# The openings and closings of two feed-forward blocks put into one written order

## The chip, the cores and the metric

One core of a Trainium2 chip. The metric is device time in microseconds (us) of one execution, the median of several runs. The core has TensorE (PE, the matmuls; PEld is its loading of weights), VectorE (DVE), ScalarE (ACT), GpSimd (POOL), and SyncE (SP), which here issues most DMAs. Each engine works through its own queue in order; semaphores hold an instruction until what it reads is there and what it overwrites has been read.

## The reference

One layer of an encoder over 768 tokens (a prompt of 512 and a sample of 256), model width 1024:

```python
def encoder_layer(x, ...):
    x = layer_norm(ALPHA * x + 0.5 * swiglu(x, ffn1_up, ffn1_down), ln1_g, ln1_b)
    u = x @ w_in
    ...                       # RWKV-7 branch h_a, retention branch h_b, gates
    x = layer_norm(ALPHA * x + mix, ln2_g, ln2_b)
    x = layer_norm(ALPHA * x + 0.5 * swiglu(x, ffn2_up, ffn2_down), ln3_g, ln3_b)
    return x

def swiglu(x, w_up, w_down):
    gate, up = jnp.split(x @ w_up, 2, axis=-1)
    return (jax.nn.silu(gate) * up) @ w_down
```

`w_up` is 1024 x 5632, `w_down` 2816 x 1024, `w_in` 1024 wide on its input side, all in float32.

## The kernel before

**Tiles.** Activations lie transposed: 128 features on the partitions, tokens along the free axis. `z[0..7]` are the eight tiles of x, 128 x 768. A float32 product is made of three matmuls on pieces: a high part (a CAST on ScalarE: xh, ph, wh, hh) and the low rest (a subtraction on VectorE: xl, pl, wl, hl), high x high, high x low and low x high. `split` makes both parts; `mmt` (L208) issues the matmuls.

**The up products.** The 2816 hidden features are 22 blocks, numbered j. A block needs a gate and an up column of weights, each in two halves of 512 inputs, against x in two halves of inputs and two halves of 384 tokens. Instead of eight half products the kernel makes seven (Strassen's way): products 1 and 2 take the gate weights as loaded and x as it is ("11", "21"); products 5, 7, 6, 3 take sums of weights (`combine`, tile sa, L359), and products 4 to 7 differences of x, the forms "T1" to "T4" (tiles f, L293, then split into xh, xl, eh, el); product 3 takes "22". Each product is 12 matmuls of 128 x 384 into a PSUM bank (tile pc). ScalarE copies or applies silu (u, L367, L374, L415, L421), VectorE adds products up (L410), multiplies gate by up (L427), and the result is split into hh (L432) and hl (L436).

**The down products.** The blocks are grouped in `CHUNKS` of 6, 6, 5 and 5. The down products of the first three groups are mixed into the up products of the next; those of the last group (`last_down`, L567 adds them to z) come at the end, first for the 512 prompt tokens ("segment 0"), then for the 256 of the sample ("segment 1"), for the eight output tiles n. The group's weights (tiles w) are loaded and split for segment 0; what still has a place is kept for segment 1, and five of the eight are loaded and split again. The first two outputs are begun before the last block's hh is there.

**The order.** `ffn` builds a list of items, one for each product. Inside `manual_schedule` the three compute engines keep the order in which `body` writes the instructions: at step t the additions of item t-1, loads for up to `AHEAD` = 9 items ahead, weight sums, then `prep(t + 2)`, which casts and subtracts the weights of item t+2, then the matmuls of item t. What stands outside, the opening and the closing, is put in order by the scheduler's own estimates of time. The opening: `first` loads x and makes the forms; `head` and `second` make products 1 and 2 of the first `LEAD` = 4 blocks, so that their matmuls run while the forms are made; the other five products of these blocks are items. The closing: `last_down`, then `layer_norm` for each segment: a sum over features by a matmul with ones (L253, L262), centring (L273), squares (L275), their sum, the root (`rsqrt`, table load L234, then L240 to L244), scaling (L281), an affine on ScalarE (L282) and, after the first block, the split into xh and xl for the next stage.

**What follows the first block.** Two products of x with `w_in` columns 12 and 13, the "lead" tiles, are begun in the closing (`project`). The next stage takes their PSUM tiles over: L703 to L707 read them into t and r, and the projections of that stage use a ring of three PSUM tiles (mm), the two lead tiles and one of their own. `mmps` counts through this ring with `self.turn`, which starts at -1, so that the first tile given out is the first lead's.

Of the kernel before, what the change touches and what calls it, by code (L numbers as in the profile page):

```python
# [18 lines left out]
P = 128  # L19
# [36 lines left out]
LEAD = 4  # L56
RAWS = 10
AHEAD = 9
# [11 lines left out]
class Builder:  # L70
# [165 lines left out]
    def rsqrt(self, p, eps, o, t, last):  # L236
        nc = self.nc
        last = self.lntable(last)
        with self.tc.issue_after(last):
            nc.scalar.activation(o, p, AF.Ln, bias=eps)  # L240
# [49 lines left out]
    def forms(self, z, xs, ext, tmp):  # L290
        nc = self.nc
        m = KT // 2
        sub = lambda o, a, b: nc.vector.tensor_tensor(out=o, in0=a, in1=b, op=ALU.subtract)  # L293
        B = [[t[:, c:c + TH] for t in (z[k], z[k + m]) for c in (0, TH)] for k in range(m)]
        ta = [tmp.tile([P, T], F32, tag="hh", name=self.nm("f")) for k in range(m)]
        for k, (b11, b12, b21, b22) in enumerate(B):
            sub(ta[k][:, :TH], b12, b11)
            self.split(ta[k][:, :TH], *(t[:, TH:] for t in xs[k]))
        tb = [tmp.tile([P, T], F32, tag="hl", name=self.nm("f")) for k in range(m)]
        for k, (b11, b12, b21, b22) in enumerate(B):  # L300
            sub(tb[k][:, :TH], b22, b12)
            self.split(tb[k][:, :TH], *(t[:, :TH] for t in ext[k]))
        for k, (b11, b12, b21, b22) in enumerate(B):
            sub(ta[k][:, TH:], b22, ta[k][:, :TH])
            self.split(ta[k][:, TH:], *(t[:, 2 * TH:] for t in ext[k]))
        for k, (b11, b12, b21, b22) in enumerate(B):
            sub(tb[k][:, TH:], b21, ta[k][:, TH:])
            self.split(tb[k][:, TH:], *(t[:, TH:2 * TH] for t in ext[k]))

    def ffn(self, ctx, z, xs, idx, up, down, after, lead, first, then=None):  # L310
# [6 lines left out]
        hs, raws, open_ = {}, {}, {}  # L317
# [25 lines left out]
        def load(j, part):  # L343
            if (j, part) not in raws:
                raws[j, part] = raw(up[j, :, part])
            return raws[j, part]

        def pieces(src):
            n = src.shape[-1]
            h, l = (fw.tile([P, m * P], F32R, tag=t, name=self.nm(t), bufs=4)[:, :n] for t in ("ph", "pl"))  # L350
            self.split(src, h, l)
            return tuple(t.rearrange("p (a b) -> p a b", b=P) for t in (h, l))

        def product(ps, w, x, start):
            self.mmt(ps, self.terms(pieces(w), X[x]), ((0, TH),), start, True, not start)

        def combine(a, b, op):
            t = fw.tile([P, m * P], F32, tag="sa", name=self.nm("sa"), bufs=4)
            nc.vector.tensor_tensor(out=t, in0=a, in1=b, op=op)  # L359
            return t  # L360

        def head(j):
            g = load(j, 0)
            s, uu = (hp.tile([P, T], F32, tag=t, name=self.nm("u")) for t in ("hh", "hl"))
            ps = self.bank()[:, :TH]
            product(ps, g[0], "11", True)
            nc.scalar.copy(uu[:, :TH], ps)  # L367
            open_[j] = s, uu, ps
            return g

        def second(j, g):
            s, uu, ps = open_[j]
            product(ps, g[1], "21", False)
            nc.scalar.activation(s[:, :TH], ps, AF.Silu)  # L374

        def pair_items(j):
            early = j in open_
            st = {}

            def sums(names):  # L380
                def run():
                    (g0, g1), (u0, u1) = load(j, 0), load(j, 1)
                    for n in names:
                        if n == 1:
                            st[1] = combine(u0, u1, ALU.add)
                        elif n == 3:
                            st[3] = combine(g0, u0, ALU.subtract)
                        elif n == 2:
                            st[2] = combine(st[1], g0, ALU.subtract)
                        else:  # L390
                            st[4] = combine(g1, st[2], ALU.subtract)
                return run

            if early:
                st["s"], st["u"] = open_[j][:2]
# [5 lines left out]
            def bank_of(n):  # L401
                key = {1: "A", 2: "A", 5: "C", 3: "C", 7: "D", 4: "D", 6: "B"}[n]
                if key not in st:
                    st[key] = self.bank()[:, :TH]
                return st[key]

            src = {1: lambda: load(j, 0)[0], 2: lambda: load(j, 0)[1], 4: lambda: load(j, 1)[1],
# [26 lines left out]
            def after_late(n):  # L434
                if n == 4:
                    nc.vector.tensor_tensor(out=hs[j][1], in0=st["s"], in1=hs[j][0].bitcast(F32), op=ALU.subtract)  # L436
                    for k in ((j, 0), (j, 1)):
                        raws.pop(k)

            items = []  # L440
            of = {5: 1, 7: 3, 6: 2, 3: 4}
            for n in (5, 7, 6, 3, 4) if early else (1, 5, 7, 6, 2, 3, 4):
# [4 lines left out]
                need = (sums((of[n],)), 3 if early else 6 + (n in (6, 3))) if n in of else None  # L447
                items.append((src[n], mm, *(lambda n=n, f=f: f(n) for f in (post, late, after_late)), need))
# [908 lines left out]
```

## Time and profile before

| what | us |
|---|---|
| median of 3 runs | 1986.06 (1985.82 to 1988.34) |
| the profiled execution | 1982.73 |
| its span | 1981.0 |
| PE busy in the span | 1886.8 |
| DVE busy | 1259.4 |
| ACT busy | 807.0 |

The profile is one execution; its span runs from the first to the last instruction, and 1.73 us lie around it. A line number names a line of the kernel, often that of a helper, so the tile beside it says what the work is. "PE pc L208 <- ACT u L367" in the table of waits means that matmuls into pc waited for ScalarE's copy of u. A number in brackets after x counts instructions. The granted clock is TensorE's, 1.00 at full speed. Times of stages: the first block runs from 0 to about 582 with its closing from about 488, the second from about 1430 to the end with its closing from about 1908.

### The profile page before, as it was taken

What the parts mean: (1) busy time and instruction counts of PE and PEld (TensorE: products, weight loads), DVE (VectorE), ACT (ScalarE), POOL (GpSimd) and SP (SyncE); (2) the same over time, 40 slices, a digit from 0 to 9 for tenths busy, and PEclk for the clock granted to TensorE, in tenths of its full rate; (3) what the DMA queues carried; (4) which work ended last, traced back from release to release, by engine and by line L of the source; (5) the groups of instructions that cost most, each with busy time, mean ns of one, the idle gap of its engine ahead of it and who ended that gap; (6) DMA issues with size and microseconds to landing.
All of it is one profiled execution on the core that took longest, in us unless ns stands there. A gap on an engine that the chain in (4) does not pass through costs nothing.

```text
span 1981.0 us, 33145 instructions
## 1 busy us (share of the span) xinstructions
PE 1886.8 (95%) x13098; PEld 1685.0 (85%) x13098; DVE 1259.4 (64%) x2208; ACT 807.0 (41%) x1521; POOL 190.3 (10%) x290
## 2 busy tenths in 40 slices
PE   7999999999989999999899989999899999999997
PEld 7999999998778778887688867789789899899985
DVE  8855746656745686768445555386797477375655
ACT  6422423323454353545255555332554234132325
POOL 0000000000000365345610000000000000000000
PEclk9999999999989999999999989999999999999998
DMA  5222222121332433333555442654222221222221
GB/s 197 81 69 75 64 75 71 49 85 45 123 103 69 156 115 127 116 128 121 155 164 139 123 121 74 210 163 138 80 77 73 81 69 56 79 63 69 67 70 66
DMA packets 140444, 198.40 MB, mean 100 GB/s; under 512 B 55552, under 2 KB 73600, under 8 KB 140288
## 3 DMA queue, kind: packets, MB, share of 16 engines
q1 hardware_dynamic: 122752, 174.25, 27.8%
q0 software_dynamic: 3424, 14.94, 2.2%
q10 hardware_dynamic: 14112, 7.08, 1.3%
q8 instruction: 104, 1.70, 0.4%
q14 instruction: 52, 0.43, 0.1%
HBM read 154.54 MB, written 41.68 MB: 99 GB/s over the span
## 4 chain that ended last, share of the span: by engine, by line
PE 82%; DVE 9%; ACT 4%; DMA 3%; issue 2%; SPq 0%; ACTq 0%; POOL 0%; DVEq 0%; POOLq 0%
PE mm L208 39%; PE pc L208 30%; PE pc L253 2%; PE mm L630 2%; PE pc L107 2%; PE pc L1046 1%; DMA t<-gd 1%; PE w L982 1%; PE pc L1094 1%; PE pc L687 1%; DVE z L281 1%; PE w L993 1%; DVE u L410 1%; PE w L987 1%; PE pc L1055 1%
## 5 line engine op out<-in xcount | busy, mean ns | idle before, releaser
L208 PE MATMUL pc<-xh,ph 128*128 128x384 f32 x704 | 241.9, 344 | 20.8 <-ACT u L367 6.7
L208 PE MATMUL pc<-xl,ph 128*128 128x384 f32 x704 | 237.8, 338 | 0.1
L197 ACT CAST ph<-wr 128x512 fp32r<-128x512 f32 (+1 forms) x232 | 131.1, 568 | 220.2 <-PE mm L208 140.3
L208 PE MATMUL mm<-xh,wh 128*128 128x512 f32 (+1 forms) x640 | 177.2, 356 | 15.0 <-DVE t L707 5.1
L410 DVE TENSOR_TENSOR u<-u,pc 128x384 f32<-128x384 f32 x220 | 121.6, 553 | 89.1 <-PE pc L208 85.4
L208 PE MATMUL pc<-el,ph 128*128 128x384 f32 x528 | 176.4, 334 | 0.0
L208 PE MATMUL pc<-eh,ph 128*128 128x384 f32 x528 | 176.4, 334 | 0.0
L208 PE MATMUL mm<-xl,wh 128*128 128x512 f32 (+1 forms) x640 | 169.9, 346 | 0.0
L208 PEld LDWEIGHTS pc<-xh,ph 128*128 128x128 f32 x704 | 133.7, 190 | 30.4 <-ACT u L367 8.0
L198 DVE TENSOR_TENSOR pl<-wr,ph 128x512 fp32r<-128x512 f32 (+1 forms) x232 | 141.6, 623 | 20.6 <-ACT ph L197 20.6
L208 PE MATMUL pc<-xh,pl 128*128 128x384 f32 x704 | 151.0, 336 | 0.0
L198 DVE TENSOR_TENSOR pl<-sa,ph 128x512 fp32r<-128x512 f32 x176 | 121.2, 689 | 45.6 <-ACT ph L197 45.4
L208 PE MATMUL mm<-hl,ph 128*128 128x512 f32 (+1 forms) x544 | 138.9, 336 | 0.0
L208 PE MATMUL mm<-hh,ph 128*128 128x512 f32 (+1 forms) x544 | 138.8, 336 | 0.0
L208 PEld LDWEIGHTS pc<-xl,ph 128*128 128x128 f32 x704 | 133.8, 190 | 0.8 <-DVE xl L198 0.7
L169 DVE TENSOR_TENSOR wl<-wr,wh 128x1024 fp32r<-128x1024 f32 (+1 forms) x68 | 74.8, 1100 | 92.7 <-PE mm L208 47.2
L208 PEld LDWEIGHTS mm<-xh,wh 128*128 128x128 f32 x640 | 101.7, 192 | 36.9 <-issue 14.9
L197 ACT CAST ph<-sa 128x512 fp32r<-128x512 f32 x176 | 105.4, 617 | 52.9 <-DVE sa L359 24.9
L208 PEld LDWEIGHTS pc<-xh,pl 128*128 128x128 f32 x704 | 125.7, 189 | 0.0
L208 PE MATMUL mm<-xh,wl 128*128 128x512 f32 (+1 forms) x640 | 124.2, 343 | 0.0
L168 ACT CAST wh<-wr 128x1024 fp32r<-128x1024 f32 (+1 forms) x68 | 62.7, 922 | 139.0 <-PE mm L208 112.7
L208 PEld LDWEIGHTS mm<-xl,wh 128*128 128x128 f32 x640 | 100.6, 192 | 16.8 <-issue 2.5
(311 smaller groups left out, 3926.3 us busy)
## 6 DMA issues: line engine op xcount, KB each, us to landing
wr<-in_f1u SPq DMA_DIRECT2D x96, 256.0 KB, 3.1
wr<-in_f2u SPq DMA_DIRECT2D x96, 256.0 KB, 3.0
wr<-in_w_in SPq DMA_DIRECT2D x30, 512.0 KB, 3.5
wr<-in_f1d SPq DMA_DIRECT2D x37, 256.0 KB, 2.7
wr<-in_f2d SPq DMA_DIRECT2D x37, 256.0 KB, 2.7
wr<-in_w_in SPq DMA_DIRECT2D x32, 256.0 KB, 3.4
dd<-ar SPq DMA_DIRECT2D x8, 768.0 KB, 3.3
dd<-kb SPq DMA_DIRECT2D x8, 768.0 KB, 4.4
```

The lines of the kernel that those rows point to most:

```text
L107: self.nc.tensor.matmul(ps, w, x[:, a:b], start=True, stop=True)
L168: nc.scalar.copy(hi, raw)
L169: nc.vector.tensor_tensor(out=lo, in0=raw, in1=hi.bitcast(F32), op=ALU.subtract)
L197: self.nc.scalar.copy(hi, src)
L198: self.nc.vector.tensor_tensor(out=lo, in0=src, in1=hi.bitcast(F32), op=ALU.subtract)
L208: self.latest = self.nc.tensor.matmul(o, w, x[:, a:b], start=start and i == 0, stop=stop and i == len(terms) - 1, skip_group_check=more).ins
L253: self.summed = nc.tensor.matmul(st["ps"], self.ones, src, start=k == 0, stop=k == KT - 1).ins
L281: nc.vector.scalar_tensor_tensor(out=zk, in0=zk, scalar=-0.5, in1=rs, op0=ALU.mult, op1=ALU.mult)
L410: add = lambda o, a, b: nc.vector.tensor_tensor(out=o, in0=a, in1=b, op=ALU.add)
L630: nc.tensor.matmul(dst, x[:, ts], w[:, :, k % 4], start=(k == 0 and q == 0), stop=(k == KT - 1 and q == 2))
L687: nc.tensor.matmul(op, v[:, a // P + j], x[:, j, :n], start=(j == 0 and q == 0), stop=(j == nj - 1 and q == 2))
L982: nc.tensor.matmul(pb[64 * h:64 * h + 64, C * j:C * j + C], sc[:, c % 4, h, 1], vu[:, c % 4, h], start=True, stop=True)
```

## The change

1. The opening of both blocks goes into the item list. `LEAD` is 6: the twelve products 1 and 2 of six blocks come first in the order `OPEN`; then the blocks go in pairs, with products 5, 7, 6 of both alternating, and then 3 and 4 of each. Product 6 of these six blocks uses an mm tile of PSUM instead of a pc bank. The gate weights are loaded half by half, in the first block mixed with quarters of x (`inputs`).
2. `forms` no longer runs at once: it returns a list of steps, and `advance(t)` writes a few of them behind each item's weights, up to three VectorE operations at a time, or more where item t needs them.
3. `prep` is split: ScalarE casts the weights of item t+3 (`high`) when VectorE makes the low part of item t+2. `AHEAD` is 10.
4. `closing` takes the place of `last_down`, `layer_norm` and the code of `project` in `first`, and is written inside `manual_schedule`. The 24 matmuls of outputs 0 and 1 that don't need the last block stand behind the last up product. The last group's weights are split once: for three outputs into hp tiles, for four into the tiles of the forms (xe, free by then), and the eighth into what is left of those. Sums, centring, squares, root, scaling and `project` are written between the products of segment 1.
5. The constants for the next stage are loaded at item 100 (`then`) instead of behind the last item. The affines of outputs 3 and 6 of segment 1 in the second block are on VectorE. `psum` starts `turn` at `len(pre) - 1`, so that the first tile given out is the pool's own, not the first lead's.

The number and the shapes of the matmuls are the same; VectorE has 17 operations fewer, ScalarE 24, SP 20 loads fewer in the first block's up weights, and 8 more in the second's.

```diff
-LEAD = 4
+LEAD = 6
+OPEN = [(1, 0), (1, 1), (1, 2), (1, 3), (2, 0), (2, 1), (1, 4), (1, 5), (2, 2), (2, 3), (2, 4), (2, 5)]
+FORMS = {True: 5, False: 6}
-AHEAD = 9
+AHEAD = 10
...
-        self.pre, self.turn = pre, -1
+        self.pre, self.turn = pre, len(pre) - 1
...
+            early = [pair_items(j) for j in range(LEAD)]
+            items += [early[j][0][n] for n, j in OPEN]
+            for j in range(0, LEAD, 2):
+                pair = early[j:j + 2]
+                fetch.setdefault(len(items), []).extend(p[1] for p in pair)
+                items += [p[0][n] for n in (5, 7, 6) for p in pair] + [p[0][n] for p in pair for n in (3, 4)]
...
+            def advance(t):
+                x = items[t][7] if 0 <= t < len(items) else None
+                names = [n for n, *_ in steps]
+                must = len(names) - names[::-1].index(x) if x in names else 0
+                begin = FORMS[own]
+                n = 0
+                while steps and (must > 0 or n < (3 if t >= begin else 0) or steps[0][0] == "11"
+                                 or steps[0][0] == "21" and t >= 0 and n < 2):
...
             def prep(t):
-                if t < len(items):
-                    ready[t] = pieces(items[t][0]())
+                if t + 1 < len(items):
+                    ready[t + 1] = high(items[t + 1][0]())
+                if 0 <= t < len(items):
+                    ready[t] = pieces(*ready[t])
...
+        def closing(out, lead):
...
+            for n in range(2):
+                ps[n] = self.mmps()
+                product(SEGS[0], n, range(nk - 1), True, False)
...
+            for n in range(KT):
+                if n == 0:
+                    add(0, KT - 1)
+                ps[n] = self.mmps()
+                product(SEGS[1], n, range(nk), True, True)
+                if n == 0:
+                    total(0)
+                elif n < 5:
+                    centre(0, 2 * n - 2)
+                    centre(0, 2 * n - 1)
+                if n > 1:
+                    total(1, n - 2)
+                if 1 < n < 6:
+                    square_sum(0, 2 * n - 4)
+                    square_sum(0, 2 * n - 3)
+                if n:
+                    add(1, n - 1)
+                if n == 5:
+                    root(0)
+                if n > 5:
+                    scale(0, 2 * n - 12)
+                    scale(0, 2 * n - 11)
+                if n == 7 and lead:
+                    low(0, 0)
+                    low(0, 1)
+            add(1, KT - 1)
+            total(1, KT - 2)
+            total(1, KT - 1)
```

VectorE at the start of the first block, before (pl: low part of a weight tile, xl: of a tile of x, f: a form):

```order
L198 TENSOR_TENSOR pl_227<-wr_119,ph_226 128x512
L198 TENSOR_TENSOR pl_244<-wr_121,ph_243 128x512
L198 TENSOR_TENSOR xl_87<-z_78,xh_86 128x384
L198 TENSOR_TENSOR xl_89<-z_79,xh_88 128x384
L198 TENSOR_TENSOR xl_91<-z_80,xh_90 128x384
L198 TENSOR_TENSOR xl_93<-z_81,xh_92 128x384
L198 TENSOR_TENSOR xl_95<-z_82,xh_94 128x384
L198 TENSOR_TENSOR xl_97<-z_83,xh_96 128x384
L198 TENSOR_TENSOR xl_99<-z_84,xh_98 128x384
L198 TENSOR_TENSOR xl_101<-z_85,xh_100 128x384
L198 TENSOR_TENSOR pl_264<-wr_147,ph_263 128x512
```

And now:

```order
L313 TENSOR_TENSOR xl_87<-z_78,xh_86 128x384
L313 TENSOR_TENSOR xl_89<-z_79,xh_88 128x384
L313 TENSOR_TENSOR xl_91<-z_80,xh_90 128x384
L313 TENSOR_TENSOR xl_93<-z_81,xh_92 128x384
L376 TENSOR_TENSOR pl_175<-wr_119,ph_163 128x512
L376 TENSOR_TENSOR pl_179<-wr_125,ph_173 128x512
L376 TENSOR_TENSOR pl_183<-wr_127,ph_177 128x512
L313 TENSOR_TENSOR xl_95<-z_82,xh_94 128x384
L313 TENSOR_TENSOR xl_97<-z_83,xh_96 128x384
L376 TENSOR_TENSOR pl_210<-wr_129,ph_181 128x512
L313 TENSOR_TENSOR xl_99<-z_84,xh_98 128x384
L376 TENSOR_TENSOR pl_244<-wr_135,ph_208 128x512
```

The low parts of the first weights now stand between the pieces of x: three gate products that need only the lower half of x come ahead of the pieces of the upper half.

VectorE at the root of segment 0 in the closing of the second block, before (z<-z,mm: a product added to z; sa: the root; z<-z,sa: scaling; z<-z,pc: centring):

```order
L242 TENSOR_TENSOR sa_19134<-sa_19133 128x512
L567 TENSOR_TENSOR z_13012<-z_13012,mm_19286 128x256
L243 SCALAR_TENSOR_TENSOR sa_19134<-pc_19100,eps,sa_19134 128x512
L244 SCALAR_TENSOR_TENSOR sa_19133<-sa_19134,sa_19133 128x512
L281 SCALAR_TENSOR_TENSOR z_13010<-z_13010,sa_19133 128x512
L281 SCALAR_TENSOR_TENSOR z_13011<-z_13011,sa_19133 128x512
L281 SCALAR_TENSOR_TENSOR z_13012<-z_13012,sa_19133 128x512
L281 SCALAR_TENSOR_TENSOR z_13013<-z_13013,sa_19133 128x512
L281 SCALAR_TENSOR_TENSOR z_13014<-z_13014,sa_19133 128x512
L281 SCALAR_TENSOR_TENSOR z_13015<-z_13015,sa_19133 128x512
L281 SCALAR_TENSOR_TENSOR z_13016<-z_13016,sa_19133 128x512
L281 SCALAR_TENSOR_TENSOR z_13017<-z_13017,sa_19133 128x512
```

And now:

```order
L243 TENSOR_TENSOR sa_19169<-sa_19168 128x512
L244 SCALAR_TENSOR_TENSOR sa_19169<-pc_19026,eps,sa_19169 128x512
L245 SCALAR_TENSOR_TENSOR sa_19168<-sa_19169,sa_19168 128x512
L602 TENSOR_TENSOR z_12954<-z_12954,mm_19148 128x256
L634 SCALAR_TENSOR_TENSOR z_12949<-z_12949,sa_19168 128x512
L634 SCALAR_TENSOR_TENSOR z_12950<-z_12950,sa_19168 128x512
L602 TENSOR_TENSOR z_12955<-z_12955,mm_19175 128x256
L634 SCALAR_TENSOR_TENSOR z_12951<-z_12951,sa_19168 128x512
L634 SCALAR_TENSOR_TENSOR z_12952<-z_12952,sa_19168 128x512
L602 TENSOR_TENSOR z_12956<-z_12956,mm_19199 128x256
L634 SCALAR_TENSOR_TENSOR z_12953<-z_12953,sa_19168 128x512
```

Before, all eight scalings of segment 0 came in a row, with two additions of segment 1 behind them. Now the additions of the last three outputs stand between the scalings, and five scalings come ahead of segment 1's centring; the other three stand behind it (not shown).

ScalarE in the closing of the first block, before (z<-z,vec: the affine; xh: the high part of the next stage's x; the rows begin at the root's last step):

```order
L241 ACTIVATE sa_4926<-sa_4926 128x512
L282 ACTIVATE z_78<-z_78,vec_4640 128x512
L282 ACTIVATE z_79<-z_79,vec_4640 128x512
L197 CAST xh_4877<-z_78 128x512
L282 ACTIVATE z_80<-z_80,vec_4640 128x512
L197 CAST xh_4879<-z_79 128x512
L282 ACTIVATE z_81<-z_81,vec_4640 128x512
L282 ACTIVATE z_82<-z_82,vec_4640 128x512
L197 CAST xh_4881<-z_80 128x512
```

And now:

```order
L242 ACTIVATE sa_5046<-sa_5046 128x512
L644 ACTIVATE z_78<-z_78,vec_2419 128x512
L647 CAST xh_4663<-z_78 128x512
L644 ACTIVATE z_79<-z_79,vec_2419 128x512
L647 CAST xh_4665<-z_79 128x512
L644 ACTIVATE z_80<-z_80,vec_2419 128x512
L647 CAST xh_4667<-z_80 128x512
L644 ACTIVATE z_81<-z_81,vec_2419 128x512
L170 CAST wh_5409<-wr_5408 128x1024
L647 CAST xh_4669<-z_81 128x512
L644 ACTIVATE z_82<-z_82,vec_2419 128x512
L199 CAST wh_5470<-wr_5469 128x1024
```

Each high part now follows its affine at once, and two casts of the next stage's weights (wh), which stood ahead of the root before, stand among them.

More of the change, by code (lines that the diff above doesn't have):

```diff
@@ L303, in forms @@
[L303 to L310, printed above, removed]
+        part = lambda ts, k, c: tuple(t[:, c:c + TH] for t in ts[k])
@@ new lines, in forms, with low, begin @@
+        if own:
+            rows += [("22", None, B[k][3], part(xs, k + m, TH)) for k in range(m)]
+        rows += [("T4", tt(tb[k], B[k][2], tb[k], ALU.subtract), tb[k], part(ext, k, TH)) for k in range(m)]
+        steps, late = [], None
+        def low(src, hi, lo):
+            return lambda: nc.vector.tensor_tensor(out=lo, in0=src, in1=hi.bitcast(F32), op=ALU.subtract)
+        for name, make, src, (hi, lo) in rows:
+            def begin(make=make, src=src, hi=hi):
+                if make:
+                    make()
+                nc.scalar.copy(hi, src)
+            if late and name == "21" != late[0]:
+                steps.append(late)
+                late = None
+            steps.append((name, begin, bool(make), False))
+            if late:
+                steps.append(late)
+            late = name, low(src, hi, lo), True, True
@@ L311, in ffn @@
+        return steps + [late]
+    def ffn(self, ctx, z, xs, idx, up, down, out, lead, start, own, then=None):
         nc = self.nc
@@ L354, in product @@
[L354 to L359, printed above, removed]
-            return t
[L362 to L374, printed above, removed]
+        def load(j, part, h):
+            if (j, part, h) not in raws:
+                raws[j, part, h], = raw(up[j, :, part, h * m:h * m + m])
+            return raws[j, part, h]
+        def high(src):
+            h = fw.tile([P, m * P], F32R, tag="ph", name=self.nm("ph"), bufs=4)[:, :src.shape[-1]]
+            nc.scalar.copy(h, src)
+            return src, h
@@ L497, in body @@
                     fetch.setdefault(len(items), []).append(get)
[L498 to L499 removed]
+                    items += [its[n] for n in (1, 5, 7, 6, 2, 3, 4)]
                     if q == 0 and ci:
[L501 to L504 removed]
+                        items += down_items(ci - 1)
@@ L539, in body @@
                 for f in afters:
                     f()
+                ahead(t)
+                if then and t == 100:
+                    with self.tc.issue_after(self.mark):
+                        then()
+                for f in extra.get(t, ()):
+                    f()
+                prep(t + 2)
+                advance(t)
+                if t > 0:
+                    items[t - 1][3]()
+                    afters = [items[t - 1][4]]
+                if 0 <= t < len(items):
+                    items[t][1](ready.pop(t))
@@ L548, in last_down @@
+        def closing(out, lead):
             ch = chunks[-1]
-            a, b = seg
-            mean = {"ps": self.bank()[:, :b - a]}
-            order = [n for n in held] + [n for n in range(KT) if n not in held]
-            now = dict(held)
+            nk = len(ch)
             x = [hs[j] for j in ch]
-            part = lambda ps, w, c, *ends: self.mmt(ps, self.terms([t[:, c] for t in w], x[c]), (seg,), *ends)
-            begun = {n: self.mmps() for n in order[:2]} if a == 0 else {}
-            for n, ps in begun.items():
-                part(ps, now[n], slice(0, len(ch) - 1), True, False)
@@ L569, in last_down @@
-            return mean, {n: now[n] for n in order[KT - (max(CHUNKS) + 2 - len(ch)):]}
-        first(load, ext, hp)
-        for j in range(lead):
-            second(j, head(j))
-            raws.pop((j, 0))
-        held = {}
-        body()
-        if then:
-            then()
-        for seg in BLK[idx]:
-            mean, held = last_down(seg, held)
-            after(seg, mean, lp)
-        def lead_weights(src):
-            return [pieces(t) for t in raw(src)]
-        return lead_weights
+            g0 = V_LN[idx]
@@ L588, in rope @@
+        if start:
+            start(load)
+        held, rest, stock = {}, [], {}
+        with self.tc.manual_schedule(engines={E.Activation, E.DVE, E.PE}):
+            body()
+            closing(out, lead)
     def rope(self, ps, hi, lo):
```

345 lines of the change are left out of this document (218 added, 127 removed).

## Prediction

> **What bounds the kernel now.** I read the page first: busy shares, then the chain that ended last.
>
> ```profile
> span 1981.0 us, 33145 instructions
> PE 1886.8 (95%) x13098; PEld 1685.0 (85%) x13098; DVE 1259.4 (64%) x2208; ACT 807.0 (41%) x1521; POOL 190.3 (10%) x290
> ...
> PE 82%; DVE 9%; ACT 4%; DMA 3%; issue 2%; SPq 0%; ACTq 0%; POOL 0%; DVEq 0%; POOLq 0%
> ```
>
> TensorE is the bound, and the change leaves its matmuls as they are in number and shape. Only time in which it idles or runs at a lower clock can be won. So I asked next for a table by stage: both feed-forward blocks cut into opening, middle and closing (window, length, then busy time with instruction count of PE, PEld, DVE, ACT and POOL, then the granted clock, the DMA share and GB/s).
>
> ```profile
> 0.00:30.00 30.00, 18.73 (x74) 17.08 (x75) 24.54 (x55) 21.92 (x44) 0.21 (x4) 0.89 0.74 254
> 30.00:90.00 60.00, 58.66 (x335) 57.41 (x334) 53.65 (x93) 23.12 (x41) 0.00 (x0) 1.00 0.30 96
> 90.00:476.00 386.00, 386.00 (x2220) 367.98 (x2219) 234.55 (x371) 125.43 (x237) 0.00 (x0) 1.00 0.22 68
> 476.00:500.00 24.00, 22.06 (x99) 18.20 (x97) 11.97 (x22) 5.18 (x12) 0.00 (x0) 0.93 0.24 68
> 538.00:582.00 44.00, 33.49 (x160) 28.00 (x159) 26.27 (x57) 26.98 (x49) 0.00 (x0) 0.84 0.32 107
> 1430.00:1455.00 25.00, 18.68 (x101) 17.44 (x102) 24.33 (x50) 20.85 (x43) 0.00 (x0) 1.00 0.11 35
> 1455.00:1500.00 45.00, 43.81 (x250) 42.86 (x249) 40.78 (x68) 17.34 (x31) 0.00 (x0) 1.00 0.32 104
> 1897.00:1915.00 18.00, 16.06 (x72) 13.33 (x71) 8.21 (x14) 4.30 (x9) 0.00 (x0) 0.91 0.12 34
> 1942.00:1965.00 23.00, 19.30 (x100) 14.13 (x99) 14.92 (x31) 14.13 (x25) 0.00 (x0) 0.95 0.25 91
> 1965.00:1981.00 16.00, 5.77 (x16) 4.37 (x16) 5.72 (x16) 8.62 (x18) 0.00 (x0) 0.61 0.21 68
> ```
>
> The middle (90 to 476) has no idle PE at all. The loss sits in the four ends, which are what the change rewrites. Third, the waits of PE there (us in total, times, longest), opening and closing of the first block, then of the second:
>
> ```profile
> PE pc L208 <- ACT xh L197: 5.8, 1, 5.8
> PE pc L208 <- ACT u L367: 4.3, 2, 3.8
> PE pc L208 <- ACT ph L197: 1.1, 1, 1.1
> ...
> PE mm L208 <- DVE t L707: 5.1, 1, 5.1
> PE pc L253 <- DVE z L567: 4.5, 1, 4.5
> PE mm L208 <- ACT hh L432: 1.7, 1, 1.7
> PE mm L208 <- DVE xl L198: 0.9, 1, 0.9
> ...
> PE pc L208 <- issue: 2.5, 1, 2.5
> PE pc L208 <- ACT u L367: 2.4, 2, 1.6
> PE pc L208 <- ACT ph L197: 1.5, 1, 1.5
> ...
> PE pc L253 <- DVE z L567: 2.7, 1, 2.7
> PE mm L208 <- ACT hh L432: 1.7, 1, 1.7
> PE pc L253 <- ACT sa L275: 1.0, 1, 1.0
> ```
>
> Three stretches, the 1.7 us wait for hh of the first block and two soon behind it, show that a wait can cost more than itself:
>
> ```profile
> 488.40:490.07 1.67, 0.00 (x1) 0.00 (x1) 0.77 (x2) 0.83 (x1) 0.00 (x0) 1.00 0.02 5
> ...
> 491.42:494.83 3.41, 3.39 (x9) 2.22 (x8) 2.60 (x5) 1.88 (x6) 0.00 (x0) 0.50 0.00 0
> 494.83:500.00 5.17, 5.17 (x25) 4.26 (x23) 3.27 (x9) 1.08 (x3) 0.00 (x0) 1.00 0.62 185
> ```
>
> Soon after it the clock is at half for 3.41 us: another 1.7 us lost. After the 2.5 and 1.6 us waits of the second opening the clock stays at 1.00, so it is not certain.
>
> **A rule weighed.** The Trainium skill, "TensorE: Matmul & The Clock Gate", Part 1, says that the clock halves after an idle window of about 3.4 us and asks for no idle gap longer than that. The length of the half-clock stretch agrees; that a gap of only 1.67 us precedes it does not. By the page, waits under 3.4 us cost no clock and the half clock behind them has another cause: the third rival below. The sum goes by the rows.
>
> **The change, part by part.** Rows that carry the prices: PE's rhythm at 384 columns (4 matmuls in 0.69 us, so 0.173 each) and at 256 (5 in 0.60, so 0.12), VectorE's operations, and its eight scalings in a row.
>
> ```profile
> 484.56 0.85 PE L208 MATMUL pc<-xh,pl 128*128 128x384 f32 x4
> 485.25 0.33 PE L208 MATMUL pc<-eh,ph 128*128 128x384 f32 x1
> ...
> 538.52 0.76 PE L208 MATMUL mm<-hh,w 128*128 128x256 f32 x5
> 539.12 0.59 PE L253 MATMUL pc<-z,ones 128*128 128x256 f32 x2
> ```
> ```profile
> L198 DVE TENSOR_TENSOR pl<-wr,ph 128x512 fp32r<-128x512 f32 x184 | 126.1, 687 | 15.5 <-ACT ph L197 15.5
> L410 DVE TENSOR_TENSOR u<-u,pc 128x384 f32<-128x384 f32 x220 | 121.6, 553 | 89.1 <-PE pc L208 85.4
> L198 DVE TENSOR_TENSOR xl<-z,xh 128x384 fp32r<-128x384 f32 x24 | 12.7, 557 | 1.0 <-ACT xh L197 1.0
> ```
> ```profile
> 8.71 1.56 DVE L198 TENSOR_TENSOR xl<-z,xh 128x384 fp32r<-128x384 f32 x3 [0.35 <-ACT xh L197]
> ...
> 1952.42 0.69 ACT L240 ACTIVATE sa<-pc,eps 128x512 f32<-128x512 f32 x1 [2.00 <-PE pc L253]
> ...
> 1956.13 0.69 DVE L244 SCALAR_TENSOR_TENSOR sa<-sa,sa 128x512 f32<-128x512 f32 x1
> 1956.85 4.91 DVE L281 SCALAR_TENSOR_TENSOR z<-z,sa 128x512 f32<-128x512 f32 x8
> ```
>
> *First opening.* Counting matmuls against 0.173 us: 0 to 30 holds 74, so 30 - 12.8 = 17.2 us are lost; 30 to 90 holds 335, so 60 - 58.1 = 1.9. Together 19.1. Afterwards twelve gate products stand ahead of everything, fed half by half (one weight tile and four pieces of x first, where two tiles came first), and the block forms are slipped between them. The start remains: 5.3 us (now 5.8). The first clock-up remains, estimated at 2.9 (between one half-clock stretch, 1.7, and the 3.3 that 0.11 of 30 us gives now plus one more, 5.0). The waits for u go, because the bank that is reused was copied a product earlier; I leave 1.4 for small ones (ph 1.1 is the nearest). What is late next is VectorE: up to the 25th weight its queue holds 25 low parts, 13 weight sums, 44 pieces of 384 (x and its forms), 10 additions of u and three of 768 (taken as 0.96). By the rhythm in the rows above (0.61 for 512; 1.00 for two steps of 384, so 0.50) that is 38 x 0.61 + 54 x 0.50 + 2.9 = 53.1 us, begun at about 4.8, so ready at 57.9; PE wants it at 5.3 + 2.9 + 24 x 12 x 0.173 = 58.0. By whole durations (0.687, 0.557, 0.553) it is 59.0 us, ready 5.8 late. I take 1.0, near the rhythm, because queued VectorE work follows it. Lost afterwards 5.3 + 2.9 + 1.4 + 1.0 = 10.6; **gain 8.5** (3.7 to 9.5).
>
> *Second opening.* Lost now: 25 - 101 x 0.173 = 7.5 and 45 - 250 x 0.173 = 1.7, together 9.2. The 2.5 us "issue" wait stays: it ends when the stage before gives up its PSUM, which the change leaves alone. Of the other 6.7, I expect to remain 2.5 for the fifth product, which needs x's upper half from ScalarE (bounds 0 and the first opening's 3.8), and 1.5 in small waits (as in the first opening); VectorE's queue has 12 operations fewer than in the first. **Gain 2.7** (0.5 to 4.5).
>
> *First closing.* Lost now: waits 1.7 + 0.3 (hl) + 4.5 + 0.9 + 5.1 = 12.5, and half clock 24 x 0.07 + 44 x 0.16 = 8.7; 21.2 in all. Afterwards the 24 begun matmuls of 512 columns (about 5 us, by the 25 in 5.17 us) stand behind the last up product instead of being mixed into it, and cover the chain from that product to hh and hl, of which 1.7 + 0.3 is bare now. New waits, walked along the written order: before the last product of the second segment, its PSUM tile waits for an addition that VectorE has behind the root: 4.4 (start of L240 to end of L244) minus the product and sum that PE still has (15 x 0.12 + 0.4) = 2.2. The last mean then waits behind four scalings of 0.61 less what PE has left: 2.1. The projection of the last two tiles waits for the low parts behind the second root: 2.4. The next stage's first product takes the third PSUM tile instead of a lead's, so the 5.1 goes; its second still wants a lead's tile: 3.9 (bounds 0 and 5.1). The two weight casts that now stand among ScalarE's affines delay these by 0 to 2. With one partly halved stretch (1.0) that is 11.6. SP loses nothing, since weights no longer reloaded leave its queue. **Gain 9.6** (4 to 15).
>
> *Second closing.* The same waits for hh and their clock go: 1.7 + 0.3 + 18 x 0.09 = 3.6. The ten re-splits of last-chunk weights in the second segment leave both engines, and 2.7 + 1.0 with 23 x 0.05 = 1.2 of clock go. In their place come 2.2 (root, as above), 0.7 and 0.4. In the tail, square sums at full clock save what two scalings, moved behind the second root, give back. 3.6 + 4.9 - 3.3 = 5.2; **gain 5.0** (1 to 8).
>
> *Middle.* ScalarE one product ahead, keeping 10 instead of 9 items fetched, and the constants' loads, moved from the end to the 100th product on SP's queue (POOL's work stays as it is): 0, hidden by PE's full 386 us; without that cover a late cast would cost its 0.6 each.
>
> Sum: 8.5 + 2.7 + 9.6 + 5.0 = 25.8. The profiled execution took 1982.73 us (span 1981.0), so 1956.9; it lay 3.3 below the median of the runs, 1986.06. **Forecast 1960.3.**
>
> **The rivals.**
> - *VectorE takes the place in the openings.* For: 24.5 of 30 and 24.3 of 25 us busy there already. Against: much of that is order, not amount. At whole durations the first opening loses 4.8 more and the second, with less in its queue, about 2: 1967.
> - *New short waits halve the clock.* Six waits of 2.1 to 3.9 us remain in my walk. For: the 1.67 us gap. Against: 1.00 between 1430 and 1455. Each 1.7, less the 1.0 counted: 9.2 more, 1969.5.
> - *Short waits were not what halved the clock.* Then the half clock behind both waits for hh (1.7 and 1.6) and in 1942 to 1965 (1.2) comes all the same: 4.5 less gain, 1964.8. For: 1.00 after the waits of 2.5 and 1.6. Against: behind both waits for hh it stands at 0.93 and 0.91 of their windows.
> - *Slower: ScalarE's cast a product too far ahead.* There are four ph tiles. The cast for product t+3 now needs the tile that product t-1 is reading; before it was that of t-2. Were each cast late, PE would wait at every product: (386 + 397) / 2.08 = 376 products' time in both middles, so 0.07 us per product eats the whole gain and at 0.1 the time is 1960 + 38 = 1998. Against: the cast has three products (6 us) and ScalarE is busy 125 of 386 us.
> - *Nothing changes.* The waits only move: same losses at other products. For: each end is a chain through ScalarE and VectorE whose length stays. 1986.
>
> **How the numbers follow.** Forecast 0.45, VectorE 0.17, new half clock 0.16, old half clock kept 0.08, slower 0.08, nothing 0.06. A change within 0.2% (4 us) can't be told from none. The first four are faster, 0.86. The range takes the forecast's own bounds that are likely together (1951 to 1966) and the three rivals above it with some spread: 1950 to 1974; the last two and the tails stay out.
>
> **What would show it.** First matmul near 5.3; no PE wait for u in the openings; no wait for hh in either closing, clock near 1.00 in 476 to 500 and 1897 to 1915; in the closings a 2 us wait for VectorE's addition after the root; the 5.1 us wait for t gone or shorter; the middles still 100% busy. I am wrong if those waits stay at their length elsewhere, or if the middles show PE idle.

## The result, and the profile after

The changed kernel takes 1955.43 us (median of 4 runs, 1954.7 to 1957.22) against 1987.2 (4 runs, 1985.82 to 1989.86): ratio 0.9849, 95% interval 0.9829 to 0.9869. The forecast was 1960.3. By the medians 31.8 us went, by the ratio 30.0. The profiled execution took 1957.22 us, 1.8 above its median; that of the kernel before lay 4.5 below the 1987.2, so the two spans differ by 25.6 only, and the stages below add up to that. The page:

```profile
span 1955.4 us, 33078 instructions
PE 1882.6 (96%) x13098; PEld 1687.1 (86%) x13098; DVE 1247.2 (64%) x2190; ACT 806.6 (41%) x1497; POOL 189.2 (10%) x290
...
PE 84%; DVE 7%; DMA 4%; ACT 3%; issue 1%; SPq 0%; ACTq 0%; DVEq 0%; POOL 0%; POOLq 0%
```

PE still bounds it, with 4 us less busy time (half clock counts as busy) and the rest of the gain out of waits. VectorE's operations are 18 fewer by the two pages (2208 and 2190), not 17. The table by stage at the places that correspond (same columns as before):

```profile
0.00:30.00 30.00, 24.62 (x118) 22.74 (x119) 19.73 (x37) 20.92 (x39) 0.21 (x4) 1.00 0.89 294
30.00:47.20 17.20, 17.18 (x100) 16.86 (x98) 17.20 (x35) 11.19 (x23) 0.00 (x0) 1.00 0.30 100
47.20:60.00 12.80, 10.60 (x52) 10.63 (x53) 12.12 (x21) 4.60 (x8) 0.00 (x0) 0.87 0.24 83
90.00:470.00 380.00, 380.00 (x2185) 361.96 (x2184) 233.40 (x385) 126.03 (x233) 0.00 (x0) 1.00 0.22 69
470.00:495.00 25.00, 24.81 (x118) 21.14 (x117) 15.56 (x29) 10.04 (x20) 0.00 (x0) 1.00 0.26 78
527.00:535.00 8.00, 5.74 (x29) 4.38 (x28) 7.63 (x14) 4.70 (x8) 0.00 (x0) 0.79 0.29 98
570.00:600.00 30.00, 30.00 (x186) 26.80 (x186) 10.98 (x17) 15.91 (x23) 0.00 (x0) 0.91 0.25 90
1440.00:1465.00 25.00, 22.31 (x113) 22.02 (x112) 23.14 (x43) 11.29 (x21) 0.00 (x0) 0.86 0.24 77
1875.00:1900.00 25.00, 24.81 (x118) 21.19 (x117) 14.93 (x27) 7.76 (x16) 0.00 (x0) 1.00 0.14 40
1925.00:1940.00 15.00, 11.95 (x66) 8.70 (x65) 7.71 (x16) 5.75 (x10) 0.00 (x0) 1.00 0.18 66
```

The first 30 us now hold 118 matmuls instead of 74. The starts of both closings (470 to 495, 1875 to 1900) run at full clock. The first middle has no idle PE (380.00 of 380 us). VectorE is the full engine in both openings (17.20 of 17.20 and 12.12 of 12.80, 23.14 of 25). The waits of PE, first opening, first closing, second opening, second closing:

```profile
PE pc L210 <- ACT xh L319: 5.4, 2, 5.1
PE pc L210 <- DVE u L414: 2.2, 1, 2.2
...
PE mm L804 <- DVE t L881: 3.1, 1, 3.1
PE mm L210 <- DVE z L602: 2.0, 2, 1.8
PE mm L210 <- DVE xl L652: 1.1, 2, 0.6
...
PE pc L210 <- DVE u L414: 2.7, 1, 2.7
PE pc L210 <- issue: 2.5, 1, 2.5
...
PE mm L210 <- DVE z L602: 2.0, 2, 1.8
PE pc L624 <- ACT wr L621: 1.1, 1, 1.1
```

The waits for ScalarE's u and for hh are gone, and both openings have one new wait, for VectorE's additions of u.

To set kernels side by side I cut each trace at marks that all of them have. The first opening goes to ScalarE's cast of the ninth block's hh, the first closing to its second reading of a projection into r; in the two traces these rows are (before, then after):

```profile
202.95 0.84 ACT L432 CAST hh<-u 128x768 fp32r<-128x768 f32 x1 [1.75 <-DVE u L427]
...
626.15 0.90 ACT L703 ACTIVATE r<-mm,vm 128x768 f32<-128x768 f32 x1 [1.78 <-PE mm L208]
```
```profile
196.90 0.83 ACT L436 CAST hh<-u 128x768 fp32r<-128x768 f32 x1 [1.58 <-DVE u L431]
...
613.07 0.90 ACT L877 ACTIVATE r<-mm,vm 128x768 f32<-128x768 f32 x1 [1.78 <-PE mm L210]
```

The projection stage goes to the scan's first matmul pc<-ar,kb; the scan, with the merge behind it, to the second block's first product; the second opening to its ninth hh; the second closing to the end. Middles are part of the closings' stretches. "Again" is a second profile of the changed kernel, taken beside later runs; the other columns are experiments below. All in us:

| stage | before | after | again | ring only | no ring | ring + closings | cast at the same step |
|---|---|---|---|---|---|---|---|
| first opening | 202.9 | 196.9 | 197.1 | 202.3 | 197.3 | 202.4 | 211.5 |
| first closing | 423.3 | 416.2 | 414.9 | 414.3 | 417.9 | 414.9 | 416.1 |
| projection | 372.5 | 362.1 | 360.6 | 360.9 | 373.6 | 363.2 | 360.9 |
| scan and merge | 433.2 | 436.3 | 437.8 | 432.2 | 439.1 | 436.6 | 432.8 |
| second opening | 191.4 | 190.7 | 189.0 | 192.4 | 189.0 | 191.5 | 199.9 |
| second closing | 357.7 | 353.2 | 353.2 | 358.1 | 352.8 | 352.6 | 353.8 |
| span | 1981.0 | 1955.4 | 1952.6 | 1960.2 | 1969.7 | 1961.2 | 1975.0 |

So 25.6 us of span went as 6.0 + 7.1 + 10.4 - 3.1 + 0.7 + 4.5. The largest piece, 10.4, lies in a stage for which the forecast had nothing. There PE waited in the kernel before, shortly ahead of the scan (950 to 990):

```profile
PE mm L208 <- DVE osq L243: 4.6, 1, 4.6
PE pc L107 <- DVE v L707: 2.3, 2, 2.1
```

and in the changed kernel (940 to 975) only

```profile
PE mm L210 <- DVE s L855: 0.7, 1, 0.7
```

The clock stood at 0.89 from 960 to 990 in the kernel before (30 x 0.11 = 3.3 us lost) and at 1.00 from 940 to 975 in the changed one. These waits and this half clock make 9.5 of the 10.4 us.

### The profile page after: what moved, and what is told of

Its sections match the earlier page's. It is cut to its first block, busy times and chain, and to the rows that moved or that the text cites. A ratio compares the mean times of both kernels' runs of the same rounds, so it can differ in the third digit from the quotient of the medians.

```text
span 1955.4 us, 33078 instructions
## 1 busy us (share of the span) xinstructions
PE 1882.6 (96%) x13098; PEld 1687.1 (86%) x13098; DVE 1247.2 (64%) x2190; ACT 806.6 (41%) x1497; POOL 189.2 (10%) x290
## 4 chain that ended last, share of the span: by engine, by line
PE 84%; DVE 7%; DMA 4%; ACT 3%; issue 1%; SPq 0%; ACTq 0%; DVEq 0%; POOL 0%; POOLq 0%
PE mm L210 40%; PE pc L210 30%; PE mm L804 2%; PE pc L109 2%; PE pc L1220 1%; DMA t<-gd 1%; PE pc L624 1%; PE w L1167 1%; PE w L1156 1%; PE pc L1268 1%; PE pc L861 1%; PE w L1161 1%; DMA wr<-in_f1u 1%; PE pc L1229 0%; PE pc L1262 0%
## 5 line engine op out<-in xcount | busy, mean ns | idle before, releaser
L210 PE MATMUL pc<-xh,ph 128*128 128x384 f32 x704 | 241.9, 344 | 12.8 <-ACT xh L319 5.4
L414 DVE TENSOR_TENSOR u<-u,pc 128x384 f32<-128x384 f32 x208 | 115.0, 553 | 121.1 <-PE pc L210 118.1
L210 PE MATMUL pc<-eh,ph 128*128 128x384 f32 x480 | 161.2, 336 | 0.0
L210 PE MATMUL pc<-el,ph 128*128 128x384 f32 x480 | 160.9, 335 | 0.0
```

The source lines that it names most:

```text
L210: self.latest = self.nc.tensor.matmul(o, w, x[:, a:b], start=start and i == 0, stop=stop and i == len(terms) - 1, skip_group_check=more).ins
L414: add = lambda o, a, b: nc.vector.tensor_tensor(out=o, in0=a, in1=b, op=ALU.add)
```

## The experiments

**The ring's start, put back and alone.** The matmuls that wait 4.6 us are gate products: they don't take the ring's next tile, but always the first lead's (`ps = self.pre[0].tile(...)`). In the kernel before, the last retention sum that the root reads (osq) lay in just that tile. The new start of the ring moves every later tile by one place.

```diff
 turn_back (from the changed kernel)
-        self.pre, self.turn = pre, len(pre) - 1
+        self.pre, self.turn = pre, -1
 turn_only (from the kernel before)
-        self.pre, self.turn = pre, -1
+        self.pre, self.turn = pre, len(pre) - 1
```

> The changed kernel with only the start of the ring of PSUM tiles put back (turn starts at -1). Theory 1 (the ring's start sets which tile the retention sums use when the gate products want the first lead's tile): the 5.1 us wait for t at the start of the projection stage comes back in place of 3.1 us, and at the change to the scan (950 to 980) PE waits 2.0 and 4.6 us again with a half-clock stretch; 6 to 10 us more than the changed kernel, 1962 to 1966, ratio to before about 0.987 to 0.990. Theory 2 (what was gained between 730 and 1410 is the order of the closing or the clock's chance): within 2 us of 1955.4, and no wait over 2 us at 950 to 980.

> The kernel before with only the start of the ring changed (turn starts at len(pre) - 1). Theory 1: the first product of the projection stage doesn't wait 5.1 us, and the waits of 2.0 and 4.6 us at 964 to 977 go; 6 to 10 us less than before, 1977 to 1981, ratio 0.995 to 0.997. Theory 2: no change, ratio 0.999 to 1.001.

Put back: 1966.98 us, ratio 0.9911 (0.9879 to 0.9942). Alone: 1963.71 us, ratio 0.9898 (0.9869 to 0.9928), so by the ratio this one line is worth about 20 us when it is changed alone, and 12 of the 30 us go when it is put back (0.9911 against 0.9849): it and the rest of the change overlap. Waits, put back and then alone; the first rows are from ahead of the scan (940 to 980), the last of each from the start of the projection stage (555 to 575, 470 to 600):

```profile
PE mm L210 <- DVE osq L244: 4.6, 1, 4.6
PE pc L109 <- DVE v L881: 2.1, 1, 2.1
...
PE mm L210 <- DVE t L881: 5.1, 1, 5.1
```
```profile
PE mm L208 <- DVE s L681: 0.7, 1, 0.7
...
PE mm L630 <- DVE t L707: 0.6, 1, 0.6
```

The wait for osq comes and goes with the line; that for t is 5.1 without it, 3.1 in the changed kernel and 0.6 alone. Theory 2 is out. Alone the kernel gains 9.0 us in the first closing and 11.6 in the projection stage, twice what I expected. Not all of the 9.0 is the ring's: up to the root of segment 1 the three engines run the same instructions in the same order as before, and yet ScalarE starts this root at 555.47 us, where it was 558.64. Less the 0.6 us from the opening, that is 2.5 us of clock (1.00 from 476 to 500, where it was 0.93) and leaves 6.5 for the ring. The two changes overlap in the first closing: the new closing without the ring saves 5.4 there (417.9), both together 7.1 and 8.4, no more than the kernel with the ring alone.

**ScalarE's cast at the same step.** Forecast: 0.

```diff
-                if t + 1 < len(items):
-                    ready[t + 1] = high(items[t + 1][0]())
-                if 0 <= t < len(items):
-                    ready[t] = pieces(*ready[t])
+                if 0 <= t < len(items):
+                    ready[t] = pieces(items[t][0]())
```

> The changed kernel with ScalarE's cast of an item's weights put back to the same step as VectorE's low part (item t+2 instead of t+3). Theory 1 (casting one product ahead is hidden, as predicted): within 1.5 us of the changed kernel on the same chip, middles 100% busy, no wait for ph or pl. Theory 2 (in the openings, where VectorE is full, each low part then waits for its cast): VectorE idles by some 0.6 us per product from 10 to 60 and 1411 to 1465, and the waits for u grow by 3 to 8 us in all.

Measured: 1979.25 us, ratio 0.9971 (0.9956 to 0.9986): all but 6 us of the gain is lost. The openings grow by 14.6 and 9.2 us, the other stages don't. PE's waits in the first 91 us (the 8.0 is the start, where the changed kernel waits 5.1 for xh), then VectorE's waits for ph there in this kernel and in the changed one, then 30 to 70 in both:

```profile
PE pc L210 <- ACT ph L369: 12.5, 6, 8.0
PE pc L210 <- DVE u L414: 4.2, 1, 4.2
PE mm L210 <- ACT ph L369: 1.7, 2, 1.4
```
```profile
DVE pl L376 <- ACT ph L369: 15.4, 16, 2.4
```
```profile
DVE pl L376 <- ACT ph L369: 3.8, 7, 1.4
```
```profile
30.00:70.00 40.00, 29.51 (x150) 26.99 (x149) 33.38 (x62) 17.33 (x36) 0.00 (x0) 0.96 0.21 69
```
```profile
30.00:70.00 40.00, 37.78 (x210) 37.49 (x209) 37.40 (x68) 19.53 (x37) 0.00 (x0) 0.96 0.29 96
```

VectorE drops from 37.40 to 33.38 of 40 us and PE from 210 matmuls to 150, with ScalarE not half busy. The low parts wait 15.4 us for their casts, where they waited 3.8, and PE waits for both; that the casts stand behind ScalarE's other work at each step is my reading of the written order. Theory 2, and more than it said.

**The cast ahead in the old kernel, and two products ahead in the new one.**

```diff
 cast_ahead (from the kernel before: the split of prep as in the changed kernel, and)
-AHEAD = 9
+AHEAD = 10
 cast_two (from the changed kernel)
-                if t + 1 < len(items):
-                    ready[t + 1] = high(items[t + 1][0]())
+                if 0 <= t + 2 < len(items):
+                    ready[t + 2] = high(items[t + 2][0]())
...
-            h = fw.tile([P, m * P], F32R, tag="ph", name=self.nm("ph"), bufs=4)[:, :src.shape[-1]]
+            h = fw.tile([P, m * P], F32R, tag="ph", name=self.nm("ph"), bufs=5)[:, :src.shape[-1]]
```

> The kernel before with only ScalarE's cast of an item's weights a product earlier (item t+3 while VectorE makes the low part of t+2), and 10 items fetched ahead. Theory 1 (the earlier cast is worth 14 and 9 us only in the new opening, where twelve gate products and the forms share ScalarE and VectorE from the first item on; the old opening has its own waits for u): openings within 2 us of before (202.9 and 191.4), rest as before, 1982 to 1987. Theory 2 (it pays in any opening, as the waits for ph of 1.1 and 1.5 us there say): openings 4 to 10 us shorter each, 1970 to 1978.

> The changed kernel with ScalarE's cast two products ahead instead of one (a fifth ph tile, sums an item earlier, 11 items fetched ahead). Theory 1 (with one product ahead no low part waits for its cast any more; what is left in the openings is VectorE's own queue): openings within 2 us of the changed kernel (196.9 and 190.7), the waits for u stay. Theory 2 (part of the waits for u is still ScalarE's): openings 2 to 6 us shorter each.

In `cast_two` the low part of product 5's weights is taken from the next sum in the first six blocks, since that sum overwrites its tile; the operations are the same in number and shape. Measured: 1988.26 us, ratio 1.001 (0.999 to 1.0029), openings 203.6 and 193.5; and 1957.53 us, ratio 0.9869 (0.984 to 0.9898), openings 199.3 and 189.4. Both are nearest to theory 1, with one opening each just beyond its 2 us (193.5 against 191.4, and 199.3 against 196.9): the cast ahead pays nothing in the old opening, is needed in the new one, and a second product ahead gains nothing. The wait left is VectorE's; with two ahead it is longer than the 2.2 us of the changed kernel:

```profile
PE pc L210 <- DVE u L414: 4.2, 1, 4.2
```

**The forms on GpSimd.** If VectorE is full, another engine could make the differences.

```diff
-        tt = lambda o, a, b, op: lambda: nc.vector.tensor_tensor(out=o, in0=a, in1=b, op=op)
+        tt = lambda o, a, b, op: lambda: nc.gpsimd.tensor_tensor(out=o, in0=a, in1=b, op=op)
```

> The changed kernel with the 16 differences of x of each opening (the forms) on GpSimd instead of VectorE. Theory (VectorE's queue is full from 22 to 58 us and alone causes the waits of 2.2 and 2.7 us for u and the half clock behind them): about 7.5 us (16 x 0.47) leave VectorE's queue in each opening, both waits and both half-clock stretches go, 6 to 9 us less, 1946 to 1950. Rival (GpSimd is slower at them or slows VectorE, and the forms come too late for products 5, 7 and 6): PE waits for xh, eh or el instead, 1955 or more.

Measured: 1962.99 us, ratio 0.9877 (0.9833 to 0.9921); openings 198.0 and 191.3, so no gain; PE waits 2.3 us for u and 1.8 for a low part, and not for the forms' pieces as the rival had it. Low parts between 17 and 47 us, in this kernel and in the changed one, and GpSimd's own operations:

```profile
L376 DVE TENSOR_TENSOR pl<-wr,ph 128x512 fp32r<-128x512 f32 x6 | 6.3, 1042 | 1.0 <-ACT ph L369 0.9
```
```profile
L376 DVE TENSOR_TENSOR pl<-wr,ph 128x512 fp32r<-128x512 f32 x6 | 4.1, 688 | 2.1 <-ACT ph L369 2.0
```
```profile
L294 POOL TENSOR_TENSOR f<-f,z 128x384 f32<-128x384 f32 x4 | 8.3, 2098 | 3.7 <-DVE el L313 3.7
```

The work leaves VectorE, but each remaining low part takes 1.04 us instead of 0.69. The Trainium skill, "SBUF — State Buffer", section "SBUF: two separate sides", offers a reason: the two engines share one port pair, which one of them holds for a whole instruction. These rows agree with it (1.04 us against 0.69); no run here looks at the ports themselves.

**The forms earlier in the second opening.** `FORMS = {True: 5, False: 6}` became `{True: 5, False: 3}`.

> The changed kernel with the second block's forms begun at item 3 instead of 6. Theory 1 (VectorE's queue alone causes the 2.7 us wait for u in the second opening; it has 5 us idle between 1411 and 1440 that earlier forms would use): the wait and the half clock behind it (0.86 of 25 us, 3.5 us) go, second opening 3 to 6 us shorter. Theory 2 (the forms then stand ahead of gate weights on both engines and only move the wait forward): the same wait at an earlier product, no gain.

Measured: 1960.96 us, ratio 0.9875 (0.9848 to 0.9902); second opening 187.3. The wait of 2.7 for VectorE's u became one of 1.8 for ScalarE's:

```profile
PE pc L210 <- ACT u L425: 1.8, 1, 1.8
```

But the same opening, in the kernel with the additions ahead (below), took 190.0, and the unchanged one 190.7 and 189.0. A gain of 3 us can't be told from the clock's play here; left open.

**The new closings with the old openings.** First with two written orders, one for the items and one for the closing, then with one:

```diff
 closing_only: the ring's start, last_raw, last_weights, closing and rsqrt of the changed kernel in the kernel before
 closing_block (from closing_only; the constants at item 100, as in the changed kernel)
-        body()
-        if then:
-            then()
         with self.tc.manual_schedule(engines={E.Activation, E.DVE, E.PE}):
+            body()
             closing()
```

> The kernel before with the changed start of the ring and the changed closings of both blocks, but its own openings, casts and constants. Theory 1 (from the marks of the runs so far: behind the ring's start the new closing gains nothing in the first block and about 5 us in the second): 3 to 5 us less than the kernel with the ring's start alone, 1958 to 1961, ratio about 0.987; what is left to the changed kernel, 4 to 6 us, is the first opening, and almost nothing the second. Theory 2 (the closings gain what the prediction said, 9.6 and 5.0, and only the noise of the clock hides it): 1949 to 1952, no more than the changed kernel.

> As the kernel with the ring's start and the new closings alone, but items and closing in one written order, as in the changed kernel, and the constants loaded at item 100. Theory 1 (the closing pays only when one order holds the begun matmuls behind the last up product; with two orders the scheduler moved them ahead again, and the 1.7 us waits for hh stayed): no wait for hh, first closing up to the second mix of r about 414 to 417 us (424.6 with two orders), second closing 352 to 354 us (359.9); 1961 to 1966 in all. Theory 2 (the new closing needs the new opening or is no better than the old one): the same 3.1 and 2.5 us waits, first closing above 420.

Measured: 1979.27 us, ratio 0.9977 (0.9961 to 0.9992), closings 424.6 and 359.9, with two orders; 1963.01 us, ratio 0.9896 (0.9879 to 0.9914), closings 414.9 and 352.6, with one. First closing with two orders and then with one:

```profile
PE mm L208 <- DVE z L577: 3.1, 1, 3.1
PE mm L208 <- DVE sa L242: 2.5, 1, 2.5
PE mm L208 <- ACT hh L431: 1.7, 1, 1.7
```
```profile
PE mm L784 <- DVE t L861: 3.1, 1, 3.1
PE mm L208 <- DVE z L580: 2.0, 2, 1.8
PE pc L591 <- DVE z L580: 1.7, 1, 1.7
```

With two orders the scheduler put the begun matmuls ahead of the last up products again (from 478.8 to 482.4, between matmuls into pc), and hh was bare. The first run had been expected at 1958 to 1961; its theory 1 fell for a reason that it had not named. Against the ring alone it is 10.3 us longer in the first closing, and 10.7 in the scan, for which no run gives the cause. The second run settles the closings: with one order they are 9.7 and 7.3 us shorter, and in the second block no constants were moved. In the first block the new closing then adds nothing to the ring (414.9 against 414.3, with 2.5 us of clock in the latter), in the second 5.5 us (352.6 against 358.1). The openings do the rest of the gain, 5.5 us in the first block.

**The additions ahead of the scalings.**

```diff
 add_first: add(1, 5) written ahead of root(0)
 adds_ahead: add(1, 5) ahead of root(0); add(1, 6) and add(1, 7) ahead of scale(0, 0) to scale(0, 3); FORMS as in forms_early
```

> The changed kernel with the addition of output 5 of segment 1 written ahead of VectorE's part of the root of segment 0 instead of behind it, in both closings. Theory (that addition alone holds the PSUM tile of the last product, which PE waits 1.8 us for in each block): both waits go, and the half clock behind the first (0.79 of 8 us, 1.7 us); 3.6 to 5.3 us less than the changed kernel, 1950 to 1952. Rival (PE only waits later, for the last mean behind the scalings): under 1 us less, with a wait of about 2 us at the last sums.

> The changed kernel with the second block's forms begun at item 3, and in both closings the last three additions of segment 1 ahead of the scalings of segment 0 (output 5 even ahead of the root). Theory 1 (in the closing the scalings between the additions hold up the last means; nothing else is late there): no wait for z before the last product and before the last sums in either closing, 2 to 4 us less in the first, 1 to 2 in the second; with the 3.4 us of the earlier forms 1949 to 1953. Rival (VectorE is full in the closing, so that the wait moves on to the low parts xl, as it moved to the last sums when only output 5 was moved): closings within 1 us of the changed kernel, 1952 to 1956.

Measured: 1959.03 us, ratio 0.9868 (0.9841 to 0.9895), closings 417.4 and 352.6; and 1960.74 us, ratio 0.9874 (0.9848 to 0.9901), closings 416.7 and 354.5. The rivals were right that the waits only move: with one addition first, to the last sums (5.8 us at the longest, where the rival had about 2), with all three, to ScalarE's xh and the squares, where the rival had named xl. First closing of `add_first`; then first and second closing of `adds_ahead`:

```profile
PE pc L613 <- DVE z L602: 6.8, 2, 5.8
```
```profile
PE mm L210 <- ACT xh L647: 3.3, 2, 2.0
...
PE pc L624 <- ACT wr L621: 3.8, 1, 3.8
```

**The changed kernel again.**

> The changed kernel once more, beside the others on the same chip. If the stage of the scan differs from run to run only by its clock: openings, closings and the projection stage within 1 us of the first profile, the scan anywhere between 432 and 443 us, total 1951 to 1962. If the first profile was an exception: openings or closings differ by over 2 us.

1956.12 us, ratio 0.9866 (0.9848 to 0.9883). All six stages lie within 1.7 us of the first profile, three of them beyond the 1 us expected. The scan and merge, whose order the change leaves alone but for single rows, ran from 432.2 to 442.9 us over all the kernels, with the granted clock. Alone with the ring, and the closings in two orders:

```profile
977.50:1409.70 432.20, 398.46 (x4598) 342.50 (x4599) 255.00 (x621) 204.98 (x479) 22.51 (x43) 0.97 0.47 142
```
```profile
989.60:1432.50 442.90, 405.45 (x4600) 348.11 (x4599) 255.71 (x622) 205.53 (x479) 22.28 (x42) 0.94 0.45 139
```

A hundredth of clock over 433 us is 4.3 us. That the clock alone makes this spread was not tested; it does mean that effects of a few us are read by stage and not from the total. No version beat the changed kernel.

## Why the prediction was right, and where it was not

The total was right (1960.3 forecast, 1955.43 measured; 25.8 us of gain summed, 25.6 in span), and the ends changed as described, but that the sum comes so near is luck: the four stages that were priced fell 7.5 us short together and the scan lost 3.1, and one stage priced at nothing gave 10.4.

- *First opening:* 8.5 forecast, 6.0 measured. The start came as written (5.1 for 5.3), the waits for ScalarE's u went. The step that was mis-sized is VectorE's queue: "I take 1.0, near the rhythm". The runs show 2.2 and a half clock behind it (12.8 x 0.13 = 1.7), so 3.9 of the rival's 5.8. VectorE ran back to back and came late at the first additions of u, six products ahead of the weight for which I had worked it out.
- *Second opening:* 2.7 forecast, 0.7 and 2.4 measured. The wait of 2.5 at the fifth product did not come; instead 2.7 for u and 25 x 0.14 = 3.5 of clock did. The remark that VectorE has 12 operations fewer there was no protection: its forms begin an item later, which I take for the reason without having shown it. The 2.5 us wait at the start stayed, and this time half clock followed it too (29 x 0.06 = 1.7 from 1411 to 1440).
- *First closing:* 9.6 forecast, 7.1 and 8.4 measured. The places came as written: hh covered and the clock at 1.00, 1.8 behind the root (2.2 forecast), 0.4 at the last mean (2.1), 1.1 for low parts (2.4), 3.1 for t (3.9). The sizes did not: all waits there came to 7.2 (3.1 + 2.0 + 1.1, and 0.6 and 0.4 that are not shown) against 10.6, but the half clock behind them (8 x 0.21 + 35 x 0.02 + 30 x 0.09 = 5.1) was priced at 1.0. What the forecast did not see is that the kernel with the third tile alone passes this stage as fast, 2.5 us of clock included.
- *Second closing:* 5.0 forecast, 4.5 measured, again with 1.8 behind the root (2.2), 0.2 at the last mean (0.7), and 1.1 at the squares (0.4).
- *Middle:* the 0 for ScalarE's earlier cast holds in the middles, whose cover is PE's full time. The step that failed is that I priced it there only. In the new openings that cover is missing, and the cast is worth 14.6 and 9.2 us. Without it the change would have been 6 us, not 30.
- *The ring's start:* the forecast followed it to the next product (5.1 us) and stopped there. The ring is used for 360 us more, and beside it stands a user that always takes the first lead's tile. That was worth another 10.4 us, the largest single term, and it covered what the other stages fell short and 3.1 us of slower scan, whose cause is open.
- *The rivals:* VectorE in the openings and the new half clock both came about in part; both are inside the measured stages. VectorE cost 2.9 more than forecast in the first opening (4.8 in the rival). Half clock in the openings and the first closing came to about 12 us in the first profile of the changed kernel, where the rival had 10.2 (9.2 and the 1.0 counted), but to about 5 in the second. The rival by which the old half clock stays did not come about: the closings start at 1.00. The runs don't settle it, though, since in the first block the kernel with the ring alone starts its closing at 1.00 with the old wait for hh (last section). Nor did the slower one: with the cast ahead the first middle stays full.

## What to carry to other kernels

When a change shifts where a round-robin of buffers starts, follow the ring to its end and look for users that take a fixed member: the gain or loss can lie hundreds of microseconds behind. Price a lead between two engines in the stage where both are full, not in the steady middle, where anything is hidden. And compare traces stage by stage at common marks; here terms of 10 us in two stages would have passed as one right total.

## What the runs showed of the hardware

A wait of about 2 us on TensorE can be followed by half clock, and need not be. Behind 2.2, 1.8 and 2.7 us in the changed kernel the clock stood at 0.87, 0.79 and 0.86 of their windows; behind 1.8 us in the second closing it stayed at 1.00. The same kernel's second profile has 1.00 behind the same 1.8 us of the first closing, and the kernel with the ring alone has 1.00 behind the 1.7 us for hh that cost the kernel before its 0.93, after the same instructions in the same order. These two rows are:

```profile
527.00:535.00 8.00, 4.53 (x30) 3.62 (x29) 7.49 (x14) 4.70 (x8) 0.00 (x0) 1.00 0.35 90
```
```profile
476.00:500.00 24.00, 21.67 (x103) 18.20 (x102) 13.28 (x25) 5.75 (x13) 0.00 (x0) 1.00 0.27 79
```

So a gain of 2 or 3 us behind such a wait can be the clock's alone. The Trainium skill, "TensorE: Matmul & The Clock Gate", Part 1, asks only for no gap longer than about 3.4 us; these rows don't bear out that a shorter one is free.

With GpSimd at work on SBUF, a VectorE subtraction of 128 x 512 took 1.04 us instead of 0.69, and GpSimd's own operations of 128 x 384 took 1.1 to 2.1 us where VectorE needs 0.55 alone (a GpSimd span is rough).
